# A loop moved between the two halves of the last expert group, weight splits in a written order, and residual adds spread out

## The chip, the cores and the metric

The kernel runs on one core of a Trainium2 chip. The metric is device microseconds per execution. The matmul engine is called PE, the vector engine DVE, the scalar engine ACT, GpSimd POOL, and SP is the engine that issues the transfers.

## The reference

Two transformer blocks on a sequence of 256 tokens of width 1024 (16 meta tokens are put in front for the first one and dropped at its end), in float32:

```python
x = first_block(x, meta_tokens, ...)   # layer norm, mixer, layer norm, experts, layer norm
return second_block(x, positions, ...) # two layers: attention and pooling, each with an MLP
```

The first block's mixer runs a gated delta rule (4 heads, chunks) and a stick-breaking attention (8 heads) side by side, gates and merges them. Its expert layer has 4 groups of 8 experts; each token goes to 2 experts of its best group, with two up matrices (1024 x 256) and one down matrix (256 x 1024) per expert, and the weighted results are added to the residual before a layer norm. The second block's first layer is attention: RMS norm, qkv product, rotation, causal softmax, output product; an MLP with squared ReLU follows (1024 to 4096 and back), then a pooling layer and a second MLP, and a last RMS norm.

## The kernel before

**Precision.** Most weights are used as two float32r numbers, a high part (ACT casts the raw weights, line 310) and a low part (DVE subtracts the high part from the raw weights, line 312), and the activations likewise (xh, xl); a product is then three matmuls: high by high, low by high, high by low (lines 360 to 362 with weights stationary, 388 to 390 with activations stationary, 372 to 400 for the versions that take all high parts first). The helper `split_into` (line 309) makes both parts. `Stream.split` (line 327) does it for a half of a 1 MB chunk: 1024 columns. `Stream.load` keeps up to N_RING = 5 chunks in flight or in store; SP issues the transfers in the order of the program. `Stream.after` may hold an instruction that the low part is to come behind. `tc.issue_after(i)` adds an edge: what is written inside comes after i on i's engine. Beyond such edges and the data's own, the compiler sets each engine's order, by the order of the text, and lets later work go ahead where it expects an engine to be idle.

**Mixer.** `delta()` (inverses of triangular matrices by `invert`, line 608: POOL masks a copy of the matrix, PE multiplies twice, DVE updates X and XT), `fill()` (the projections, one block of weights per step) and `stick()` are generators, and a loop steps them in rounds, counted by `it` (line 1016). At round 2 it writes `router_weights()` (line 952; two products of 128x288 on POOL, four matmuls on PE at line 960, small sums on DVE), at round 12 `residual_rows()` (line 557; four adds and products of 128x1024 on DVE that scale the residual by the embedding norm's gain and bias, line 561). `mark["POOL"]` is the last first product of an inverse, `mark["DVE"]` the last update of an XT; both blocks are queued behind the mark of their engine.

**Experts.** The experts' weights come as 99 chunks of 1 MB into 22 slots; a slot's next load is issued when the chunk in it has been used. There are 8 groups of 4 experts with 32 tokens each. Per group (loop from line 1425): eight chunks give gate and up (line 1441), ACT and DVE form the hidden rows, PE transposes them (line 1470), hT is copied out, and four chunks give the down products in two halves of 512 columns (line 1417). `weighted` (line 1393) scales a half by the router's weight into a high part on ACT (line 1398) and a low part on DVE (line 1400), in one buffer each; `scatter` (line 1403) adds it to the four accumulators on PE (line 1407). Experts with more than 32 tokens have further blocks. One is done in the middle, with its own weights; the others are done in a loop of the program whose count is read on the chip (`n_ext`), line 1480. In front of the last group's down products PE does WARM2 = 18 matmuls on the identity (line 483), then comes the loop, then both halves. All engines meet at the loop, and what is written behind it starts behind it. With these inputs its count is zero.

**Changeover.** Behind the last scatter PE does WARM3 = 10 matmuls on the identity; DVE takes the statistics of the accumulators (lines 446, 447), an inverse root (lines 413 to 422), ACT and DVE normalise (lines 1527, 1528), PE transposes (line 1553), ACT writes xh (line 1557), ACT and DVE in turn x (lines 1098 and 1096), DVE xl (line 1559). The second block's weights are taken in with `wpost.ahead()` (line 1537): five chunks are loaded and two halves split, the low parts behind the last normalised row `rows2`. The first quarter of qkv takes two halves with `xs_front` (line 392: all high parts first, 16 matmuls at line 400, then 8 with the low parts) and two with `xs_half`.

## Time and profile before

| | |
|---|---|
| median of 3 runs | 1025.97 us (1024.57 to 1027.17) |
| the profiled execution | 1022.95 us, span of its instructions 1021.2 us |
| PE busy | 945.9 us, 93% of the span |
| DVE, ACT, POOL busy | 590.5, 449.5, 71.0 us |
| moved by DMA | 227.39 MB, 223 GB/s on average |

The rows below are from that profiled execution. In a chain of waits each step is followed back from the last instruction to what released it; "issue" is time in which an engine waited for nothing that the profile shows. In a timeline, the bracket is the idle time of the engine ahead of the instruction and what ended it. The granted clock is a share of full speed, 2.4 GHz.

### The profile page before, as it was taken

Reading aid. Unit: us, or ns where it says so; the run is one execution under the profiler, and the core shown is the slowest. Engines: PE = TensorE matmul, PEld = TensorE weight load, DVE = VectorE, ACT = ScalarE, POOL = GpSimd, SP = SyncE. Lnnn points to the kernel's source line nnn. Section 1 sums busy time; section 2 is a strip of 40 time slices with the busy share of each in tenths; the row PEclk is TensorE's granted clock in tenths of the full one; section 3 lists DMA queues with packets and bytes.
Section 4 is the critical chain, followed back from the end, with each engine's and each line's share of the span. In section 5 each row is a group of like instructions: output and inputs, shape, how many; then the busy total and the mean of one; then the engine's idle time right before and its main releaser. Section 6 shows DMA issues by size and latency. Waiting matters only on the chain.

```text
span 1021.2 us, 15933 instructions
## 1 busy us (share of the span) xinstructions
PE 945.9 (93%) x6447; PEld 780.5 (76%) x6447; DVE 590.5 (58%) x1141; ACT 449.5 (44%) x771; POOL 71.0 (7%) x62
## 2 busy tenths in 40 slices
PE   6987998999999888888879999999999989999996
PEld 5986987899884523334367889999999889999995
DVE  7975757684764311122276777655565686565654
ACT  4943655344432111111154665544444464445442
POOL 0014232000300000000020001000000020000002
PEclk9998999999999999999989999999999999999999
DMA  9521212749779999999865534555455525555521
GB/s 361 188 96 42 83 43 83 287 163 348 305 298 381 416 426 422 427 422 426 340 234 186 178 122 164 190 172 201 169 202 173 198 84 206 173 199 171 200 83 41
DMA packets 34236, 227.39 MB, mean 223 GB/s; under 512 B 3937, under 2 KB 4705, under 8 KB 7665
## 3 DMA queue, kind: packets, MB, share of 16 engines
q1 hardware_dynamic: 34160, 226.36, 58.1%
q8 instruction: 51, 0.84, 0.3%
q14 instruction: 25, 0.20, 0.1%
HBM read 225.29 MB, written 1.05 MB: 222 GB/s over the span
## 4 chain that ended last, share of the span: by engine, by line
PE 72%; DVE 10%; DMA 10%; ACT 4%; POOL 2%; issue 2%; SPq 0%; POOLq 0%; ACTq 0%; DVEq 0%
DMA wexp<-in_wexp_dram 10%; PE bank L362 10%; PE bank L361 9%; PE bank L360 9%; PE acc L1763 5%; PE acc L1764 5%; PE acc L1765 5%; PE bank L1441 3%; DVE wsplit L312 3%; PE bank L389 3%; PE bank L390 2%; PE bank L388 2%; PE bank L1223 2%; PE bank L1417 1%; PE bank L636 1%
## 5 line engine op out<-in xcount | busy, mean ns | idle before, releaser
L312 DVE TENSOR_TENSOR wsplit<-wraw,wsplit 128x1024 fp32r<-128x1024 f32 x222 | 277.6, 1251 | 165.3 <-ACT wsplit L310 165.2
L310 ACT CAST wsplit<-wraw 128x1024 fp32r<-128x1024 f32 x222 | 231.9, 1045 | 153.0 <-PE acc L1765 90.9
L362 PE MATMUL bank<-xl,wsplit 128*128 128x256 f32 x512 | 143.7, 281 | 3.5 <-DVE xl L1543 3.5
L361 PE MATMUL bank<-xh,wsplit 128*128 128x256 f32 x512 | 143.1, 280 | 0.0
L360 PE MATMUL bank<-xh,wsplit 128*128 128x256 f32 x512 | 143.1, 280 | 0.0
L1763 PE MATMUL acc<-wsplit,mhh 128*128 128x512 f32 x256 | 100.4, 393 | 0.0
L1764 PE MATMUL acc<-wsplit,mhh 128*128 128x512 f32 x256 | 99.8, 390 | 0.0
L1765 PE MATMUL acc<-wsplit,mhl 128*128 128x512 f32 x256 | 99.7, 390 | 0.0
L362 PEld LDWEIGHTS bank<-xl,wsplit 128*128 128x128 f32 x512 | 96.4, 188 | 4.3 <-DVE xl L1543 4.3
L361 PEld LDWEIGHTS bank<-xh,wsplit 128*128 128x128 f32 x512 | 96.3, 188 | 0.5
L360 PEld LDWEIGHTS bank<-xh,wsplit 128*128 128x128 f32 x512 | 96.3, 188 | 0.5
L360 PE MATMUL bank<-hh,wsplit 128*128 128x256 f32 (+1 forms) x304 | 88.7, 292 | 0.0
L361 PE MATMUL bank<-hh,wsplit 128*128 128x256 f32 (+1 forms) x304 | 86.9, 286 | 0.6 <-DVE wsplit L312 0.6
L362 PE MATMUL bank<-hl,wsplit 128*128 128x256 f32 (+1 forms) x304 | 86.5, 285 | 0.0
L1753 ACT ACTIVATE relu<-bank 128x256 f32<-128x256 f32 x64 | 24.5, 383 | 85.5 <-PE bank L362 85.5
L1441 PE MATMUL bank<-wexp,xt 128*32 128x512 f32 x512 | 62.2, 598 | 0.0
L361 PEld LDWEIGHTS bank<-hh,wsplit 128*128 128x128 f32 x304 | 57.4, 189 | 1.1 <-DVE wsplit L312 0.8
L360 PEld LDWEIGHTS bank<-hh,wsplit 128*128 128x128 f32 x304 | 57.5, 189 | 0.3 <-issue 0.2
L362 PEld LDWEIGHTS bank<-hl,wsplit 128*128 128x128 f32 x304 | 57.3, 189 | 0.0
L1765 PEld LDWEIGHTS acc<-wsplit,mhl 128*128 128x128 f32 x256 | 48.0, 188 | 10.1
L1764 PEld LDWEIGHTS acc<-wsplit,mhh 128*128 128x128 f32 x256 | 48.1, 188 | 9.9 <-DVE wsplit L312 0.3
L1763 PEld LDWEIGHTS acc<-wsplit,mhh 128*128 128x128 f32 x256 | 48.1, 188 | 9.6
(535 smaller groups left out, 1635.6 us busy)
## 6 DMA issues: line engine op xcount, KB each, us to landing
wexp<-in_wexp_dram SPq DMA_DIRECT2D x99, 1024.0 KB, 19.5
wraw<-in_wpost_dram SPq DMA_DIRECT2D x81, 1024.0 KB, 4.7
wraw<-in_wpre_dram SPq DMA_DIRECT2D x30, 1024.0 KB, 4.9
h<-in_x_dram SPq DMA_DIRECT2D x2, 512.0 KB, 4.2
eb<-in_rowv_dram SPq DMA_DIRECT2D x2, 512.0 KB, 11.2
out_dram<-of SPq DMA_DIRECT2D x4, 256.0 KB, 2.1
cpre<-in_cst_dram SPq DMA_DIRECT2D x1, 915.5 KB, 10.4
pmat<-in_poolm_dram SPq DMA_DIRECT2D x1, 544.0 KB, 3.6
```

What stands on the lines that cost most here:

```text
L310: S.copy(hi, src)
L312: (sub or V).tensor_tensor(lo, src, hi.bitcast(F32), op=OP.subtract)
L360: PE.matmul(p[:, :width], wh[:, o:o + 128], xh[:, k, :], start=k == 0, stop=False)
L361: PE.matmul(p[:, :width], wl[:, o:o + 128], xh[:, k, :], start=False, stop=False)
L362: PE.matmul(p[:, :width], wh[:, o:o + 128], xl[:, k, :], start=False, stop=k == nk - 1)
L388: PE.matmul(banks[c], xh[:, k, tsl], w1, start=k == 0, stop=False)
L389: PE.matmul(banks[c], xh[:, k, tsl], w2, start=False, stop=False)
L1441: PE.matmul(pg[32 * e:32 * e + 32, :], xt[:, k, 32 * e:32 * e + 32], w[:, e, :], start=k == 0, stop=k == 7)
L1753: S.activation(t, p[:, :SEQ], AF.Relu)
L1763: PE.matmul(ac[c][n], hh_, wh, start=g == 0 and k == 0, stop=False)
L1764: PE.matmul(ac[c][n], hh_, wl, start=False, stop=False)
L1765: PE.matmul(ac[c][n], hl_, wh, start=False, stop=g == 7 and k == 3)
```

## The change

Seven edits. (1) The loop for further blocks, with its warm-up, moves from in front of the last group's first down half to between the halves; inside its body one buffer gets another tag. (2) WARM2 goes from 18 to 8, WARM3 from 10 to 16. (3) `split_into` takes two marks, one for the high and one for the low part. (4) At the start of the second block five chunks are loaded but none split; four halves are split inside the loop that makes xh, x and xl: the high parts of the first two behind the last scaling of an expert result (`mark["ACT"]`), of the other two behind the fourth xh, the low parts behind the second, fourth, sixth and eighth xl. (5) The two router products go from POOL to DVE and lose their mark. (6) The residual adds become four steps, one in each round from 8 on, each behind `mark["DVE"]`. (7) `mark["POOL"]` is gone.

```diff
--- before.py
+++ after.py
@@ -35,8 +35,8 @@
 HEADS = "32 s0 36 s1 42 s2 p0 44 s3 p1 46 s4 50 s5 p2 52 v0 p3 s6 54 s7 v1 p4 56 v2 p5 60 v3 p6 p7 v4 v5 v6 v7"
 WARM0 = 10
 WARM = 14
-WARM2 = 18
-WARM3 = 10
+WARM2 = 8
+WARM3 = 16
 PAD = 32
 N_LAST1 = 2
 N_LAST2 = 4
@@ -306,9 +306,10 @@
         nc.sync.dma_start(t, dram[i])
         return t
 
-    def split_into(hi, lo, src, sub=None, after=None):
-        S.copy(hi, src)
-        with tc.issue_after(after.ins) if after else nullcontext():
+    def split_into(hi, lo, src, sub=None, after=(None, None)):
+        with tc.issue_after(after[0].ins) if after[0] else nullcontext():
+            S.copy(hi, src)
+        with tc.issue_after(after[1].ins) if after[1] else nullcontext():
             (sub or V).tensor_tensor(lo, src, hi.bitcast(F32), op=OP.subtract)
 
     class Stream:
@@ -316,7 +317,7 @@
 
         def __init__(self, dram, n_chunks, g_halves=(), extra={}, still=()):
             self.g_halves, self.extra, self.depth, self.still = g_halves, extra, 2, still
-            self.after = None
+            self.after = (None, None)
             self.dram, self.i, self.n, self.raw, self.q, self.got = dram, 0, n_chunks, [], [], 0
 
         def load(self, n):
@@ -524,9 +525,9 @@
     for i, src in enumerate(rows):
         n = src.shape[0]
         front = rescale(src, src, mv3[:n, i, 0:1], r3[:n, i:i + 1], i == 1)
-    wpre.after = front
+    wpre.after = (None, front)
     wpre.split()
-    wpre.after = None
+    wpre.after = (None, None)
     pk = [bank("pk") for _ in range(4)]
     pm = bank("pk")
     for c in range(2):
@@ -559,6 +560,9 @@
         for c in range(2):
             for q in range(2):
                 V.tensor_tensor(h0[:, c, :], h0[:, c, :], eb[:, q, :], op=OP.add if q else OP.mult)
+                yield
+
+    residual_steps = residual_rows()
 
 
     wab = mix.tile([128, 288], F32R, tag="At0", name="wab")
@@ -613,7 +617,7 @@
         w3 = lambda t: t.rearrange("p (h d) -> p h d", d=128)
         bc = lambda m: C(m)[:, None, :].to_broadcast([128, n, 128])
         t0 = mix.tile([128, W], F32, tag=f"inv_t{n}", name="inv_t", bufs=2)
-        mark["POOL"] = G.tensor_tensor(w3(t0), w3(At), bc("lev1"), op=OP.mult)
+        G.tensor_tensor(w3(t0), w3(At), bc("lev1"), op=OP.mult)
         V.tensor_tensor(w3(XT), bc("ident"), w3(t0), op=OP.subtract)
         yield
         p = bank()
@@ -955,7 +959,7 @@
         k36 = lambda a: a.rearrange("p (k n) -> p k n", n=36)
         for q, n in enumerate(("ln1g", "ln1b")):
             o = _VCOLS[n][0]
-            G.tensor_tensor(k36(t[:, q, :]), k36(wrt), colv[:, o:o + 8, None].to_broadcast([128, 8, 36]), op=OP.mult)
+            V.tensor_tensor(k36(t[:, q, :]), k36(wrt), colv[:, o:o + 8, None].to_broadcast([128, 8, 36]), op=OP.mult)
             p = bank()
             PE.matmul(p[:, :288], C("ones"), t[:, q, :], start=True, stop=True)
             V.tensor_reduce(rcb[:, q, :], p[:, :288].rearrange("p (k n) -> p n k", n=36), axis=AX.X, op=OP.add)
@@ -1015,11 +1019,10 @@
     it = 0
     while m_on or f_on or sticks:
         if it == 2:
-            with tc.issue_after(mark["POOL"].ins):
-                router_weights()
-        if it == 12:
+            router_weights()
+        if it >= 8:
             with tc.issue_after(mark["DVE"].ins):
-                residual_rows()
+                next(residual_steps, None)
         it += 1
         if m_on:
             m_on = next(M, "end") != "end"
@@ -1330,7 +1333,7 @@
         V.tensor_copy(pm, pp[:CAP, :SEQ])
         return xx, pm
 
-    def spare_block(xx, pm, weights):
+    def spare_block(xx, pm, weights, loop=False):
 
         pg = bank2()
         for k in range(8):
@@ -1346,7 +1349,7 @@
         hT = rt([2, CAP], "xhT")
         S.copy(hT.rearrange("p q s -> p (q s)"), pt[:, :2 * CAP])
         for n in range(2):
-            ys = moe.tile([128, 512], F32, tag="ys" + "hl"[n], name="xys")[:CAP]
+            ys = moe.tile([128, 512], F32, tag="xt" if loop else "ys" + "hl"[n], name="xys")[:CAP]
             w = weights(4 + n)
             py = bank2()
             for q in range(2):
@@ -1366,7 +1369,7 @@
             spare_weights(t, eg, ej, 2 * i, 2)
             return t
 
-        spare_block(xx, pm, weights)
+        spare_block(xx, pm, weights, True)
 
 
     first, place = [], []
@@ -1395,7 +1398,7 @@
         yh = moe.tile([128, 512], F32R, tag="ysh", name="ysh")
         yl = moe.tile([128, 512], F32R, tag="ysl", name="ysl")
         for sl, p in parts_:
-            S.activation(yh[:, sl], p, AF.Copy, scale=Pw)
+            mark["ACT"] = S.activation(yh[:, sl], p, AF.Copy, scale=Pw)
         for sl, p in parts_:
             V.scalar_tensor_tensor(yl[:, sl], p, Pw, yh[:, sl].bitcast(F32), op0=OP.mult, op1=OP.subtract)
         return yh, yl
@@ -1471,14 +1474,6 @@
         hT = moe.tile([128, 2, 128], F32, tag="hT", name="hT")
         evac(hT, pt[:, :256].rearrange("p (q s) -> p q s", s=128))
         full, hf = slice(0, 512), (slice(0, 256), slice(256, 512))
-        if g == NG - 1:
-
-            warm(WARM2)
-            wx = slot()
-            with tc.issue_after(last_load[0].ins):
-                n_x = nc.values_load(n_ext[0:1, 0:1], min_val=0, max_val=14)
-            with tc.For_i(0, n_x, 1):
-                overflow(wx)
         py = bank2()
         for i in range(2):
             down(py, full, hT, chunk(), i)
@@ -1492,6 +1487,13 @@
             flush()
             pend.append((g, 1, Pm, weighted([(full, py)], Pw)))
         else:
+
+            warm(WARM2)
+            wx = slot()
+            with tc.issue_after(last_load[0].ins):
+                n_x = nc.values_load(n_ext[0:1, 0:1], min_val=0, max_val=14)
+            with tc.For_i(0, n_x, 1):
+                overflow(wx)
             py = [bank2()[:, :256], bank2()[:, :256]]
             for i in range(2):
                 w = chunk()
@@ -1533,9 +1535,7 @@
     post = ctx.enter_context(tc.tile_pool(name="post", bufs=1, reuse_waits="tile"))
     cvp.append(ctx.enter_context(tc.tile_pool(name="cvt2", bufs=2, reuse_waits="tile")))
     wpost = Stream(A["wpost"], 81, still=STILL)
-    wpost.after = rows2
-    wpost.ahead()
-    wpost.after = None
+    wpost.load(N_RING)
 
     def scaled(x, k, gname, xh, xl):
 
@@ -1554,10 +1554,16 @@
                      h0[:, c, k * 128:(k + 1) * 128], ident)
     pk = [pk[k // 2][:, (k % 2) * 256:(k % 2 + 1) * 256] for k in range(8)]
     for k in range(8):
-        S.activation(xh[:, k, :], pk[k], AF.Identity, bias=gb2[:, 1, k:k + 1], scale=gb2[:, 0, k:k + 1])
+        x3 = S.activation(xh[:, k, :], pk[k], AF.Identity, bias=gb2[:, 1, k:k + 1], scale=gb2[:, 0, k:k + 1])
         affine(k + 1, x[:, k, :], pk[k], col("ln2g", k), col("ln2b", k))
-        V.scalar_tensor_tensor(xl[:, k, :], x[:, k, :], col("nmix0", k), xh[:, k, :].bitcast(F32),
-                               op0=OP.mult, op1=OP.subtract)
+        low = V.scalar_tensor_tensor(xl[:, k, :], x[:, k, :], col("nmix0", k), xh[:, k, :].bitcast(F32),
+                                     op0=OP.mult, op1=OP.subtract)
+        if k % 2:
+            wpost.after = (mark["ACT"] if k < 4 else high, low)
+            wpost.split()
+        if k == 3:
+            high = x3
+    wpost.after = (None, None)
     dump("h2", x)
     if stop <= 2:
         return
```

## Rows read from the trace of the kernel before

**Rows 1.** Windows by stage, all engines: busy us (instructions), granted clock, DMA share, GB/s.
```profile
60.00:306.00 246.00, 233.31 (x1747) 215.91 (x1751) 158.26 (x311) 116.40 (x194) 47.69 (x38) 0.97 0.46 176
306.00:503.00 197.00, 171.54 (x1204) 76.00 (x1196) 50.97 (x148) 29.20 (x63) 0.00 (x0) 1.00 0.99 411
503.00:538.00 35.00, 25.28 (x145) 18.99 (x146) 22.23 (x43) 18.72 (x29) 6.83 (x4) 0.90 0.67 255
538.00:1021.00 483.00, 468.92 (x3008) 425.00 (x3006) 307.11 (x515) 245.86 (x402) 15.53 (x12) 1.00 0.46 163
```

**Rows 2.** Waits of PE, 60 to 306 us: total, times, longest us.
```profile
PE bank L960 <- POOL wr L958: 5.6, 1, 5.6
PE bank L636 <- ACT inv_u L632: 3.7, 2, 3.3
```

**Rows 3.** Chain of waits around the router weights: start us, us, what.
```profile
86.20 2.40 PE bank L960 x4
...
90.73 1.32 PE bank L621 x9
```

**Rows 4.** Timeline of DVE, 84 to 92 us: start, us, instruction, idle before.
```profile
85.55 1.14 DVE L617 TENSOR_TENSOR XT<-cst,inv_t 128x512 f32<-128x512 f32 x1 [0.84 <-POOL inv_t L616]
...
88.38 1.21 DVE L312 TENSOR_TENSOR wsplit<-wraw,wsplit 128x1024 fp32r<-128x1024 f32 x1
...
90.87 0.46 DVE L964 TENSOR_TENSOR wrt<-wr,rcb 128x288 f32<-128x288 f32 x1
```

**Rows 5.** Line L561, the residual adds: ns min/median/max, first and last start.
```profile
L561 DVE TENSOR_TENSOR h<-h,eb x4: 1210/1640/2314, 154.8 to 161.3; 128x1024 f32<-128x1024 f32 x4
```

**Rows 6.** Chain of waits behind the residual adds.
```profile
164.21 1.01 DVE sbwork L884 x2
```

**Rows 7.** Timeline of DVE, 130 to 156 us.
```profile
146.16 1.02 DVE L889 SCALAR_TENSOR_TENSOR sbwork<-sbwork 128x832 f32<-128x832 f32 x1 [4.47 <-ACT sbwork L887]
```

**Rows 8.** Chain of waits, 290 to 540 us.
```profile
481.56 21.26 DMA wexp<-in_wexp_dram
502.82 1.39 issue
504.21 3.65 PE bank L1417 x48
...
510.34 0.75 ACT ysh L1398 x2
...
514.22 1.09 DVE wsplit L312
...
520.21 2.27 DVE wsplit L312 x2
...
523.84 5.98 PE bank L400 x18
```

**Rows 9.** Timeline, 498 to 524 us, all engines.
```profile
498.51 4.18 PE L483 MATMUL bank<-cst 128*128 128x128 f32 x36
498.72 0.42 DVE L1092 COPY hT<-bank 128x256 f32<-128x256 f32 x1 [0.53 <-PE bank L1470]
...
505.95 1.43 PEld L1417 LDWEIGHTS bank<-wexp,hT 128*32 128x32 f32 x28 [0.30 <-issue]
...
506.20 0.69 ACT L1398 ACTIVATE ysh<-bank,pwt 128x512 fp32r<-128x512 f32 x1 [8.47 <-PE bank L1417]
506.92 0.75 DVE L1400 SCALAR_TENSOR_TENSOR ysl<-bank,pwt,ysh 128x512 fp32r<-128x512 f32 x1 [7.78 <-ACT ysh L1398]
...
508.35 1.99 ACT L310 CAST wsplit<-wraw 128x1024 fp32r<-128x1024 f32 x2 [1.46 <-DMA wraw<-in_wpost_dram]
```

**Rows 10.** Windows of PE in the changeover: busy us (instructions), granted clock, DMA share.
```profile
512.00:514.00 2.00, 2.00 (x8) 0.50 1.04 438
...
524.00:528.60 4.60, 4.60 (x14) 0.63 0.80 328
528.60:536.00 7.40, 7.40 (x34) 1.00 0.14 24
```

## What the change is predicted to do

> **What bounds the kernel now.** I read the stretches by stage first, to see which engine or queue each stage has to wait for [rows 1]. In the first block's mixer (60 to 306 us) PE is busy 233 of 246 us, the DMA less than half. In the expert stage (306 to 503) the DMA share is 0.99 and PE has 25 us to spare. In the changeover to the second block (503 to 538) PE is busy 25.3 of 35 us and the DMA share is 0.67, so neither fills it. From 538 on PE is busy 469 of 483. So time won before 306 is kept: the 22 slots for expert weights are full by then, and the next loads start when the first expert matmul frees one; the weights' stream, which fills the next 197 us, moves with that matmul. Inside the expert stage nothing can be won on an engine. In the changeover everything won is kept, as PE has hardly a gap behind it.
>
> Then the waits of PE in the mixer: two hold 8.9 us, the four products of the router weights (L960) that wait 5.6 us for POOL's L958, and L636 that waits 3.3 us for ACT [rows 2]. Last the chain of waits of the changeover [rows 8]: the last expert weights land at 481.56 + 21.26 = 502.82; 1.39 us "issue" is the loop for further blocks, which runs no time here; PE does all down products behind it; and then the chain runs over casts and subtractions of second-block weights (L310, L312) that nothing needs yet.
>
> **The change, part by part.**
>
> *Router weights (mixer).* The two products go from POOL, behind the inverses' first products, to DVE, free in order. PE did L960 at 86.20 and reached the next block of matmuls at 90.73 + 1.32 = 92.05 [rows 3]. What is late next: the transposes of XT (L621) need L617, done at 86.7, and the block's low weights need L312, done at 89.6 [rows 4]. L617 took 1.14 us next to POOL and its wait for POOL ended at 85.55, so with POOL free the transposes can end about 88.2, and L312 is done between 88.4 and 89.6. Two products on DVE cost about 2 x 0.46 us (estimate by the 128x288 product L964 [rows 4]). Bounds: 0 (the products stall PE as long elsewhere) to 5.6 us; I take 2.3, since L312 is the nearest thing that holds.
>
> *Residual rows (mixer).* The same four adds of 128x1024, 1.21 to 2.31 us each, 6.8 us in all (1.21 + 2 x 1.64 + 2.31), stood together from 154.8 to 162.5 [rows 5], and the chain passes through them to L884 at 164.21 [rows 6], then over the stick's ACT and POOL steps to PE's 3.3 us wait. Now one stands behind each of four earlier rounds, where DVE has holes such as the 4.47 us before 146.16 [rows 7]: costed at nothing by that cover, up to 4 x 1.1 us if they meet POOL's products instead. L884 can come up to 3 us sooner. Bounds 0 to 3.3; I take 2.3. Mixer: 4.6 us.
>
> *Loop between the halves.* hT is there at 498.72 + 0.42 = 499.14, but PE does the warm-up (36 instructions in 4.18 us) and waits for the loop [rows 9]. The first half's products take 505.95 - 504.21 = 1.74 us; now they run before the loop, while the last chunk is still landing. That chunk, 502.82, and the loop's 1.39 us remain [rows 8]. The loop is a wait for all engines, so behind it in each queue stand SP's five weight loads (as before), and now in front of it stand the scaling and the subtraction of the first half, 0.69 + 0.75 us [rows 9]. With the half's products first on PE they end at 499.14 + 1.74 + 0.25 (from the products to ACT, 505.95 to 506.20) + 1.44 = 502.6, before the landing: free. With the eight warm-up matmuls (16 x 0.116 us) first, at about 504: the loop passes 1.1 us later. I take 0 and keep -1.1. Gain 1.7.
>
> *Casts in a written order.* After the loop, ACT's two casts (L310) waited for the first second-block weights and ran 508.35 to 510.34; the second half's scaling followed them at once [rows 8, 9], though its buffer was free by about 508.8 (estimate: the first half's subtraction ends at 507.67 [rows 9], and four matmuls of some 0.25 us read its result). Now the casts stand behind that scaling: 1.5 us (bounds 0 to 2.0). They still wait for the same landing, and behind them on ACT stands the normalisation, needed at about 513; the casts end at 510.4, and cover it with 2 us to spare. The scatter of the second half then follows without PE's pause; it ran at a granted clock of 0.50 [rows 10]: 0.4 us (0 to 0.8).
>
> *Low parts.* Two subtractions (1.09 us each, the first at 514.22) stood between the statistics and the reciprocal root: 2.2 us. Two more, 2.27 us from 520.21, stood ahead of the first x rows: 2.0 us [rows 8]. All four are now written behind the second, fourth, sixth and eighth xl. There they lengthen DVE's work for x and xl by 4.5 us. PE's first quarter of qkv is 48 matmuls at 7.40/34 = 0.218 us [rows 10], 10.5 us; it could go on only at 523.84, with the first xl [rows 8], and ended at 536, 13.5 us after the first x row could start (520.21 + 2.27 = 522.5). Now it takes at least 12.5 (10.5, and some 2 until the first two rows are made) and at most 18 (13.5 and all four low parts). The low clock of 524 to 528.6 cost 4.6 x 0.37 = 1.7 us of the old 13.5 [rows 10] and should go, so I take 14.3: -0.8 (bounds +1 to -4.5). WARM3 at 16 ends some 3.7 us behind the scatter, just as the first transposes are ready: 0 (-1.6 if the clock is low).
>
> The tuple argument, the buffer name in the loop's body and the load of five chunks without splits change nothing that runs here: the first split keeps its edge, the body is not entered, and the same five loads leave behind the same loop.
>
> Sum of the changeover: 1.7 + 1.5 + 0.4 + 2.2 + 2.0 - 0.8 = 7.0 us. With the mixer 11.6 us: 1022.95 - 11.6 = 1011.35 us for the profiled execution, whose span is 1021.2 us. That execution is 3.0 us below the median of the runs, 1025.97; from the median the forecast is **1014.4 us**.
>
> **A rule against the row.** One and the same add takes 1.21 to 2.31 us [rows 5]. The Trainium skill, SBUF — State Buffer, section "SBUF: two separate sides", says that a DVE operation with two SBUF inputs and a POOL operation hold the shared ports in turn, each blocking the other for a whole instruction; that spread fits it. What it would make of the change is rival B.
>
> **The rivals.**
>
> B. *The mixer gives little.* Products and adds on DVE meet POOL's L616 and L626; each meeting costs 0.9 to 1.1 us in the inverse's chain, and PE's two waits only move. Four or five of them leave about 1 us of the 4.6: 1025.97 - 7.0 - 1.0 = 1018.0. For it: the add's two lengths. Against: DVE's holes.
>
> C. *The changeover gives little.* The loop passes 1.1 us late, behind the first half's scaling, and the four low parts between the xl hold PE for their whole 4.5 us: 7.0 - 5.6 = 1.4 us are left: 1025.97 - 4.6 - 1.4 = 1020.0. For it: PE already waited for xl at 523.84. Against: the first 16 matmuls need only high parts.
>
> D. *Slower: the clock.* The granted clock, 1.00 in 528.6 to 536, was 0.63 in the stretch before [rows 10], after PE had waited for the normalisation. With 8 in place of 18 warm-up matmuls PE can come out of the loop at 0.5. The Trainium skill, TensorE: Matmul & The Clock Gate, section "What's actually happening", says that low is the resting state and only activity lifts it; the row agrees. At half rate the first half (1.7), the second (1.9), eight scatter matmuls (2.0), the transposes (2.0) and the first quarter (10.5) cost another 18.1 us, less the 2.7 that low clock cost before (2.0 x 0.5 + 4.6 x 0.37): 15.4 - 11.6 = 3.8 us slower, 1029.8. It decides only if the clock stays at 0.5 through 536; a short spell costs 1 or 2 us.
>
> E. *The order isn't what the text says.* An edge only says what an instruction comes after; the compiler may put other casts or the products where they hold as before. Then only the moved half's 1.7 us are left: 1024.3.
>
> **How the numbers follow.** Forecast 0.55, B 0.18, C 0.12, D 0.06, E 0.09. What a measurement can tell from no change is 0.3%, 3.1 us: under 1022.9 is faster, over 1029.0 slower. Faster 0.55 + 0.18 + 0.12 = 0.85, same 0.09, slower 0.06. The forecast's own range is 1009 to 1018 (mixer up to 8.9 us, changeover up to 10, not both at their ends); with B and C inside it is 1009 to 1021.5.
>
> **What would show it.** Right: PE's waits for L958 and before L636 each under 1 us and the first expert matmul 4 to 5 us earlier; the first half's products before the loop; the second half's scaling with no L310 ahead; no L312 between statistics and root; first x row some 7 us sooner after the last landing; PE at full clock from the first quarter on. Wrong: a wait of PE for DVE in 80 to 150 us in place of POOL's; the last landing no earlier; DVE's last xl later than 13 us after the first x row; a clock of 0.5 in the first quarter.

## The result: 1014.33 us, a ratio of 0.990

The changed kernel took 1014.33 us (median of 4 runs, 1013.32 to 1017.42) beside 1025.27 us for the kernel before (4 runs). The ratio is 0.9896, with an interval of 0.9868 to 0.9923: 10.7 us less, beyond the 0.3% that a measurement can tell. Six more runs of the same kernel, on the chip of the last experiments, gave 1017.44 us and 0.9926 (0.9908 to 0.9944), 7.6 us less. All ten have a median of 1017.1 us. The range (1009 to 1021.5) holds for both groups. That the first median lies 0.1 us from the forecast of 1014.4 is luck: the median of all ten lies 2.7 us above it, and two terms were off in opposite directions.

**The profile after.** The profiled execution took 1015.25 us, its span 1013.5. First the windows by stage, all engines, as in [rows 1]:

```profile
60.00:301.00 241.00, 230.09 (x1751) 213.04 (x1755) 159.82 (x314) 116.64 (x195) 46.33 (x36) 0.99 0.48 180
301.00:498.00 197.00, 171.34 (x1200) 74.10 (x1192) 50.98 (x148) 29.32 (x63) 0.00 (x0) 1.00 0.99 411
498.00:526.00 28.00, 19.90 (x130) 14.46 (x126) 21.40 (x41) 17.33 (x28) 5.39 (x4) 1.00 0.65 252
```

The mixer is 5 us shorter, the expert stage as long as before, and the changeover up to the products of the root ends 28 us behind the expert stage, not 35 (these products also stand ten matmuls earlier on PE than before, as told below). The mixer's waits of PE, 60 to 306 us (total, times, longest us), against [rows 2]:

```profile
PE bank L625 <- DVE XT L621: 3.8, 2, 3.1
PE bank L640 <- ACT inv_u L636: 2.1, 2, 1.5
```

PE no longer waits for POOL's router products; 3.8 us came back as two waits for XT, the thing named as late next. (The same list also has 3.9 us for `krow`. That is no loss of the change: the longest of these waits, 2.6 us, is as long in the kernel before and ends there at 59.0 us, just outside the window.) Of the 3.3 us ahead of L636 (now L640) 0.61 us are left at that place; the rest of the 2.1 is an earlier wait that grew from 0.4 to 1.5 us; the account of the residual rows comes back to it.

The timeline of the changeover (start, us, instruction, idle before), against [rows 8, 9]:

```profile
494.31 1.07 PE L1420 MATMUL bank<-wexp,hT 128*32 128x512 f32 x8 [0.52 <-DVE hT L1095]
495.31 2.05 PE L484 MATMUL bank<-cst 128*128 128x128 f32 x16
497.29 1.07 PE L1420 MATMUL bank<-wexp,hT 128*32 128x512 f32 x8
498.47 0.69 ACT L1401 ACTIVATE ysh<-bank,pwt 128x512 fp32r<-128x512 f32 x1 [5.62 <-PEq L1495]
499.19 0.75 DVE L1403 SCALAR_TENSOR_TENSOR ysl<-bank,pwt,ysh 128x512 fp32r<-128x512 f32 x1 [4.93 <-ACTq L1495]
500.70 0.49 PE L1410 MATMUL acc<-ysh,Pm 128*128 128x512 f32 x1 [2.35 <-DVEq L1495]
...
503.76 0.84 ACT L1401 ACTIVATE ysh<-bank,pwt 128x256 fp32r<-128x256 f32 x2 [4.60 <-PE acc L1410]
...
506.10 1.99 ACT L311 CAST wsplit<-wraw 128x1024 fp32r<-128x1024 f32 x2 [1.50 <-DMA wraw<-in_wpost_dram]
...
510.04 1.52 DVE L1530 TENSOR_SCALAR h<-acc,mv,rs_y 128x512 f32<-128x512 f32 x2
```

The last expert weights land at 498.03. The first half's products run before the loop, as written, but the 16 warm-up instructions stand between their two steps: the half ends 2 us later than need be, DVE's subtraction ends at 499.94, and PE leaves the loop 2.68 us behind the landing; before, it was 1.39 [rows 8]. The second half's scaling then runs with no cast ahead, and no low part stands between statistics and normalisation.

What comes next, on DVE (timeline) and on POOL (timeline):

```profile
512.34 1.00 DVE L1099 TENSOR_SCALAR x<-bank,colv 128x256 f32<-128x256 f32 x2 [0.78 <-ACT xh L1557]
...
514.88 1.23 DVE L313 TENSOR_TENSOR wsplit<-wraw,wsplit 128x1024 fp32r<-128x1024 f32 x1
...
520.94 1.21 DVE L313 TENSOR_TENSOR wsplit<-wraw,wsplit 128x1024 fp32r<-128x1024 f32 x1
522.08 1.50 DVE L1559 SCALAR_TENSOR_TENSOR xl<-x,colv,xh 128x256 fp32r<-128x256 f32 x1
523.50 3.94 DVE L313 TENSOR_TENSOR wsplit<-wraw,wsplit 128x1024 fp32r<-128x1024 f32 x2
```
```profile
519.41 1.33 POOL L1579 TENSOR_TENSOR acc<-sq 128x512 f32<-128x512 f32 x1 [250.74 <-ACT sq L1574]
521.79 1.51 POOL L1579 TENSOR_TENSOR acc<-acc,sq 128x512 f32<-128x512 f32 x1 [1.05 <-ACT sq L1574]
523.38 1.33 POOL L1587 TENSOR_TENSOR acc<-acc,sq 128x512 f32<-128x512 f32 x1
524.78 1.58 POOL L1589 TENSOR_TENSOR acc<-acc 128x256 f32<-128x256 f32 x1
```

DVE has no hole from the first x row on. In the compiled order its fourth low part, at 520.94, is that of the fifth half of weights; the fourth half's, which the first quarter needs, is the one at 523.50. Beside POOL's sums a low part takes up to 2.28 us (the first of the two at 523.50) in place of 1.23, and an xl 1.50 in place of 0.48. PE's wait for POOL's sums (497 to 545 us; first the kernel before, then the changed one) and its windows in the changed kernel (busy, granted clock, DMA share, GB/s):

```profile
PE bank L1596 <- POOL acc L1583: 1.1, 1, 1.1
```
```profile
PE bank L1602 <- POOL acc L1589: 3.8, 1, 3.8
```
```profile
513.00:522.70 9.70, 9.25 (x38) 1.00 0.72 258
526.50:530.60 4.10, 4.10 (x13) 0.58 0.88 302
530.60:536.00 5.40, 5.40 (x25) 1.00 0.64 220
```

The compiler put the root's four products ten matmuls earlier than before (behind 38 of the quarter's 48), PE waits 3.75 us there for POOL's sums, and behind the wait it runs at a granted clock of 0.58: another 4.1 x 0.42 = 1.7 us. In the kernel before, the last of POOL's sums stands in the chain of waits as

```profile
535.61 1.60 POOL acc L1583
```

It ends at 537.21, 14.8 us behind the first x row (522.40); in the changed kernel the sums end at 526.36, 14.0 us behind it. So the sums came no later behind that row. PE came sooner: its 38th matmul is done 10.3 us behind the row, and there it has to wait.

### The profile page after: what moved, and what is told of

Its sections match the earlier page's. It is cut to its first block, busy times and chain, and to the rows that moved or that the text cites. A ratio compares the mean times of both kernels' runs of the same rounds, so it can differ in the third digit from the quotient of the medians.

```text
span 1013.5 us, 15919 instructions
## 1 busy us (share of the span) xinstructions
PE 941.8 (93%) x6439; PEld 775.4 (77%) x6439; DVE 593.1 (59%) x1143; ACT 449.1 (44%) x771; POOL 68.3 (7%) x60
## 4 chain that ended last, share of the span: by engine, by line
PE 45%; DVE 3%; ACT 2%; POOL 0%; issue 0%; ACTq 0%; DVEq 0%
PE bank L363 7%; PE bank L362 6%; PE bank L361 6%; PE acc L1769 6%; PE acc L1770 6%; PE acc L1771 6%; PE bank L391 2%; PE bank L390 2%; PE bank L389 2%; DVE wsplit L313 1%; ACT wsplit L311 1%; DVE xl L1543 0%; PE bank L1648 0%; PE bank L1612 0%; PE bank L1659 0%
## 6 DMA issues: line engine op xcount, KB each, us to landing
cpre<-in_cst_dram SPq DMA_DIRECT2D x1, 915.5 KB, 10.3
```

## The experiments

All medians, in the order run (10 runs where no number is given); "before" was 1025.25, 1024.5 and 1025.44 us beside the three groups of four.

| run | median us (runs) | ratio to before | interval |
|---|---|---|---|
| mix_only | 1018.89 (10) | 0.9939 | 0.9920 to 0.9959 |
| chg_only | 1022.35 | 0.9970 | 0.9952 to 0.9988 |
| loop_only | 1022.56 | 0.9976 | 0.9957 to 0.9995 |
| order_only | 1022.88 | 0.9978 | 0.9964 to 0.9992 |
| root_later | 1017.49 (6) | 0.9923 | 0.9907 to 0.9939 |
| warm_last | 1016.12 (6) | 0.9929 | 0.9905 to 0.9953 |
| both | 1015.35 (5) | 0.9908 | 0.9894 to 0.9923 |
| no_warm | 1015.69 (4) | 0.9906 | 0.9887 to 0.9925 |
| all_three | 1014.82 (6) | 0.9897 | 0.9879 to 0.9915 |
| after_again | 1017.44 (6) | 0.9926 | 0.9908 to 0.9944 |
| router_only | 1022.95 (10) | 0.9968 | 0.9948 to 0.9989 |
| resid_only | 1020.47 (5) | 0.9956 | 0.9932 to 0.9981 |

One kernel's runs lie 2.6 to 8.2 us apart, so the traces have to tell single terms. This table is read from one trace each: the first expert matmul and the last expert weights' landing (us from the start), and, in us behind that landing, where PE leaves the loop, the first x row (DVE), the first product with pT in the second block's attention (PE), and the end.

| trace | first expert matmul | landing | loop left | first x row | pT | end |
|---|---|---|---|---|---|---|
| before | 305.61 | 502.82 | 1.39 | 19.58 | 93.04 | 518.37 |
| after | 300.73 | 498.03 | 2.68 | 14.31 | 90.52 | 515.42 |
| after_again | 300.58 | 497.88 | 2.69 | 14.31 | 90.45 | 515.59 |
| mix_only | 302.88 | 499.98 | 1.53 | 19.25 | 91.86 | 516.97 |
| chg_only | 307.58 | 505.90 | 1.63 | 13.26 | 89.41 | 514.53 |
| loop_only | 305.51 | 502.18 | 3.34 | 19.71 | 90.90 | 515.99 |
| order_only | 308.38 | 506.24 | 0.74 | 13.90 | 90.09 | 514.98 |
| root_later | 304.56 | 502.43 | 2.04 | 13.69 | 89.69 | 514.78 |
| both | 302.47 | 500.15 | 1.47 | 12.65 | 89.76 | 515.38 |
| all_three | 300.22 | 497.55 | 1.68 | 12.87 | 88.62 | 513.75 |
| warm_last | 297.31 | 494.41 | 6.93 | 18.12 | 94.33 | 519.94 |
| no_warm | 300.69 | 498.32 | 4.00 | 17.55 | 92.33 | 517.47 |
| router_only | 306.36 | 504.25 | 0.74 | 20.31 | 92.41 | 517.58 |
| resid_only | 301.87 | 499.15 | 3.55 | 21.29 | 93.88 | 519.55 |

**The mixer's edits alone.**

```diff
-            G.tensor_tensor(k36(t[:, q, :]), ...)
+            V.tensor_tensor(k36(t[:, q, :]), ...)
...
-        if it == 12:
+        if it >= 8:
             with tc.issue_after(mark["DVE"].ins):
-                residual_rows()
+                next(residual_steps, None)
```

> Only the mixer's edits (router products on DVE, residual adds one per round); the changeover stays as before. Theory: they give about 4.6 us, kept through the expert stage: 1025.3 - 4.6 = 1020.7 us, the first expert matmul 4 to 5 us earlier than in the trace before, and the changeover from the last landing on as long as before. Rival: most of the 4.9 us between the two traces is chance of the granted clock in the first 25 us and in the router stage: then 1.5 to 2.5 us, 1023 to 1024, with PE's 5.6 us wait replaced by waits for XT.

6.2 us by the ratio (0.0061 x 1025.25), 4.2 to 8.2 by its interval: the theory's mechanism, and by the median more than its 4.6, which the interval still holds.

**The changeover's edits alone** (loop between the halves, warm-ups, written order of the splits; the two runs below divide it).

```diff
-    wpost.after = rows2
-    wpost.ahead()
+    wpost.load(N_RING)
...
+        if k % 2:
+            wpost.after = (mark["ACT"] if k < 4 else high, low)
+            wpost.split()
```

> Only the changeover's edits (loop between the halves, new warm-up counts, written order of the splits); the mixer as before. Theory: 7.0 us less what the changed trace shows to be given back, 2.7 us more of PE's wait for the second block's root sums: about 5 us, 1020.5, the span from the last landing to the end of the first quarter some 6 us shorter. With the mixer's part it adds up to the whole change (10.9 us). Rival: the two parts don't add, as the mixer's gain is chance: then this one alone gives 9 or more, 1016.

3.1 us (1.2 to 4.9): under the 5 expected here, under the prediction's 7.0, and well under the rival's 9. The first x row comes 6 us sooner behind the landing than before, but at pT 3.6 us are left of it.

**The loop's move and the warm-ups alone.**

```diff
-WARM2 = 18
-WARM3 = 10
+WARM2 = 8
+WARM3 = 16
...
-        if g == NG - 1:
-            warm(WARM2)
...
         else:
+            warm(WARM2)
```

> Only the loop between the halves with the new warm-up counts; the first splits as before (in the compiler's order). Theory: the first half's 1.74 us leaves the path, but the loop waits for its scaling and passes 1.2 us later, and the casts still hold ACT in front of the second half's scaling: 0 to 1 us, 1024.3 to 1025.3. Rival: the moved half is worth its full 1.7 us or more: 1023 or less.

2.5 us. The median is the rival's, but not by a sooner second half: PE leaves the loop 1.95 us later behind the landing than before, and the first x row is not earlier (19.71 against 19.58). The gain stands behind that row, where the profile shows no wait of PE for xl and none for the root. Matmul by matmul against the trace of before, 0.9 us come at the first weights of the quarter, but the three traces with the old changeover (mix_only, router_only, resid_only) have those too; another 1.4 us come at the root's products, where POOL's sums end 11.9 us behind the first x row, not 14.8. Why they end sooner there stays open.

**The order of the splits alone.**

```diff
+        with tc.issue_after(after[0].ins) if after[0] else nullcontext():
+            S.copy(hi, src)
+        with tc.issue_after(after[1].ins) if after[1] else nullcontext():
```

> Only the written order of the first four splits; the loop in front of both halves and the old warm-up counts. Theory: casts and low parts leave the chain: 1.5 + 2.2 + 2.0 us, of which the wait for the root sums takes back about 2.5: 3 to 4 us, 1021.5 to 1022.3. Rival: without the moved loop the order gives nothing, since ACT then waits for the first landing in any case: 1024.5 or more.

2.3 us (0.8 to 3.7), a little under the theory's smallest gain. The first x row comes 5.7 us sooner; then PE waits 3.79 us at the root's products, as in the changed kernel. So this wait belongs to the written order, not to the loop's move.

**The root's products ten matmuls later.**

```diff
-                xs_half(wpost, k0, 8, xh, xl, pb)
+                done = xs_half(wpost, k0, 8, xh, xl, pb)
...
-                rs[:] = rstd_columns(acc)
+                with tc.issue_after(done.ins): rs[:] = rstd_columns(acc)
```

> The changed kernel, with one edge more: the four products that sum the squares for the second block's root come behind the last matmul of the quarter's step before, ten matmuls later on PE, at the place that they have in the kernel before. In the trace of the changed kernel PE waits 3.75 us for POOL's sums at these products and its matmuls behind them run 0.43 us apart for some 4 us. Theory (this wait is where the changeover's gain is given back): the ten matmuls of 0.22 us fill 2.2 us of the wait, about 1.5 us of it stay, and the spell at the low clock (1.7 us) goes with it or shrinks: 1010.4 to 1012.1 us against 1014.3 for the changed kernel. Rival (the wait is only in front of the next limit, the evictions that need the root): PE waits behind the products instead, 1014 to 1016 us.

The median says no gain and lies above both ranges expected. PE's waits, 497 to 545 us, and a window of PE in that run:

```profile
PE bank L390 <- DVE wsplit L313: 3.2, 1, 3.2
```
```profile
529.60:534.50 4.90, 4.90 (x16) 0.65 0.80 264
```

The wait at the root is gone, and PE stands nearly as long at its 39th matmul, for the fourth half's low part on DVE; the low clock follows again. The root was not the bound: DVE's work stands right beside POOL's (the low part ends 13.4 us behind the first x row, the sums 14.0), and the theory's 2.2 to 3.9 us fall.

**The warm-up behind the half's last product; and both edges.**

```diff
-            warm(WARM2)
+            with tc.issue_after(mark["PE"].ins): warm(WARM2)
```

> The changed kernel with the warm-up behind the first half's last product, where the text has it; in the trace of the changed kernel it stands between the two steps of that half (2.05 us), the half ends at 498.36, its subtraction on DVE at 499.94, and PE leaves the loop 2.67 us behind the last landing, 1.28 us later than before the change. Theory: the half ends about 2 us sooner, the loop waits for the landing alone and is left some 1.4 us behind it: 1.2 to 1.3 us gained, 1013.0 us. Rival (the loop's passing is hidden anyway, or PE loses the same in clock because the warm-up now ends while PE waits): 1014.3 us, no change; in that case PE's work behind the loop starts sooner and the first x row does not.

> The changed kernel with both edges, the later root products and the warm-up behind the first half's last product. Theory: the two gains stand in different stretches and add: 2.2 to 3.9 and 1.2 us, so 1009.2 to 1010.9 us, the fastest of all these kernels. Rival: the sooner loop only lengthens the wait for POOL's sums or the other way round, and one of the two gains is lost: 1012 to 1013 us.

Both lie above what was expected, and neither median separates from the changed kernel's. (The trace of the first has a spell of half clock in the expert stage, told of in the last section, so its loop is left late.) In the trace with both, the loop is left 1.47 us behind the landing and the first x row comes 1.66 us sooner than in the changed kernel (12.65 against 14.31). Not all of this is the edge: without it the loop is left 7.3 us behind the last hidden rows' transposes, with it 6.4 to 6.5, whenever the weights land, so the edge is worth 0.8 to 0.9 us and not 1.2. The warm-up itself now stands last ahead of the loop: PE's first matmul behind the loop comes 1.5 to 1.6 us after its end. More than half of the 1.66 us is lost again at once: PE waits 3.2 us for the low part as above, and the clock stays low for longer, in the window of PE

```profile
526.30:532.00 5.70, 5.70 (x16) 0.50 0.79 276
```

**No warm-up in the changeover.** Both counts 0; matmuls on the identity are left out that nothing reads.

> The changed kernel without the two warm-ups of the changeover (8 at the loop, 16 behind the scatter; their matmuls write nothing that is read). Theory (the price of rival D is a short spell): PE comes out of the loop at the low clock and the second half (1.9 us), the scatter (2.0 us) and the transposes (2.0 us) run at half rate until the clock rises; less the 2.05 us of warm-up that stood ahead of the loop: 2 to 5 us slower than the changed kernel, 1016 to 1019 us. Rival (as D was priced, low clock through the first quarter): 1026 us or more. A third outcome, 1014 us or less, would say that the warm-ups buy nothing here.

1015.69 us: in none of the three ranges, 0.3 us under the theory's and 1.7 over the third outcome. Beside the changed kernel's 1014.33 and 1017.44 no price shows. The windows of PE show the low clock and how short it is:

```profile
503.00:508.00 5.00, 4.34 (x36) 0.66 0.92 341
508.00:514.00 6.00, 1.30 (x4) 0.69 1.01 426
514.00:518.00 4.00, 3.94 (x19) 0.61 0.73 303
518.00:526.00 8.00, 7.00 (x31) 1.00 0.56 197
```

From 518 on, with the first quarter hardly begun, the clock is full. Behind the landing the trace is 1.8 us later at pT than the changed kernel; against the spread of runs that is nothing measurable. The run doesn't price the warm-ups alone. Its last hidden rows' transposes come 196.4 us behind the first expert matmul, not 192.6, after a spell of half clock in the expert stage, and its loop is left only 5.2 us behind them, not 7.3. Its compiled order differs too: the root's products stand behind all 48 matmuls, PE waits 2.24 us there, and behind that wait the clock stays full. So from the first x row to pT it takes 74.8 us, 1.4 less than in the changed kernel.

**All three edges.** Beside both edges above, the fifth half's cast and low part come last; `LOW[1]` is the last square and `LOW[0]` the low part of the fourth half:

```diff
-        mean_square(x, k, acc)
+        with tc.issue_after(x3.ins) if k == 5 else nullcontext():
+            mean_square(x, k, acc)
+    wpost.after = (LOW[1], LOW[0])
```

> The changed kernel with the later root products and the late warm-up (as in the run with both), and one order more: the cast and the low part of the fifth half of second-block weights, which the compiler put between the seventh and the eighth xl, ahead of the low part of the fourth half, come behind the last square and behind that low part; the third square comes behind the eighth xh, where it stood. In the run with both PE waits 3.2 us for the fourth half's low part, and half the clock is granted for some 6 us behind the wait. Theory (what gives the changeover's gain back is DVE's work behind the first x row, and the order in it): the fourth low part starts 1.2 us sooner and runs clear of some of POOL's sums (2.28 us beside them, 1.2 alone), so the wait shrinks by 1.2 to 2.2 us and the low clock by up to 2 us: 1011.2 to 1014.1 us against 1015.35. Rival (PE waits for the next low part or for POOL's sums by as much, or the clock falls as before): 1014.5 to 1016 us, no difference.

DVE's timeline, and PE's waits, 497 to 545 us:

```profile
518.14 1.54 DVE L1561 SCALAR_TENSOR_TENSOR xl<-x,colv,xh 128x256 fp32r<-128x256 f32 x2
519.60 1.22 DVE L315 TENSOR_TENSOR wsplit<-wraw,wsplit 128x1024 fp32r<-128x1024 f32 x1
521.17 4.10 DVE L315 TENSOR_TENSOR wsplit<-wraw,wsplit 128x1024 fp32r<-128x1024 f32 x2 [0.35 <-ACT wsplit L313]
```
```profile
PE bank L1604 <- POOL acc L1591: 2.5, 1, 2.5
```

The fourth half's low part now runs 9.2 us behind the first x row, not 11.2, and takes 1.22 us. PE no longer waits for it; it has done all 48 matmuls where it waits for POOL's sums, 2.5 us. pT comes 1.1 us sooner behind the landing than with both, 1.9 sooner than in the changed kernel. So the theory holds for the wait that it named, and the rival for what came next: most of it is now the wait for the sums, and the low clock behind it is as in the changed kernel (0.58 for 4.1 us). The median, 1014.82 us, is in the rival's range; it is 2.6 us below the changed kernel's in the same group, but the intervals of the two ratios overlap, so it is the fastest of that group and not shown to be faster.

**The changed kernel once more.** No edit.

> The changed kernel once more, unaltered, for more runs of it beside the others. If its gain of 10.7 us (four runs, interval 7.9 to 13.5) is what the traces add up to, 1014 to 1016 us; if the runs with one edge more (1015.35 to 1017.5) truly lost time, it stays at 1014.3 or under and below them; if they only drew from the same spread, it comes out between 1015 and 1016.5 us. First expert matmul by the traces of six kernels with the mixer's change: 297.3 to 304.6 us.

1017.44 us: above all three expectations. The trace is the same as the first (300.58 and 14.31 against 300.73 and 14.31), so the first four runs drew from the lower part of the spread, and the runs with one edge more lost nothing.

**Each of the mixer's edits alone** (the two hunks above).

> The kernel before with the two router products on DVE, free in order, and nothing else. Theory: PE's wait of 5.6 us for POOL's L958 goes, and about 3.5 us of it come back as a wait for DVE's L617 and the transposes behind it: 2.1 to 2.3 us, 1023.0 us; PE's wait ahead of L636 (3.3 us) stays. Rival B: PE waits as long at 80 to 150 us, 1024.5 to 1026 us.

> The kernel before with the four residual adds one to a round and nothing else. Theory: PE's wait ahead of L636 falls from 3.3 to under 1 us, 2.3 to 2.7 us, and some of the spell of low clock behind it (0.88 granted over 176 to 190 us) goes too: 1021.0 to 1023.0 us. Rival B: the adds meet POOL's products and lengthen the inverses' chain by 1 us each: 1024.5 to 1026 us.

3.3 us (0.0032 x 1025.44) and 4.5 us, each with an interval of 2 us or more either way; their sum, 7.8, is above the 6.2 of both together, within these intervals. PE's waits of 60 to 306 us, first with the router products alone, then with the residual rows alone:

```profile
PE bank L621 <- DVE XT L617: 3.8, 2, 3.1
PE bank L636 <- ACT inv_u L632: 3.7, 2, 3.3
```
```profile
PE bank L963 <- POOL wr L961: 5.6, 1, 5.6
...
PE bank L639 <- ACT inv_u L635: 0.6, 1, 0.6
```

Each edit takes away its own wait and leaves the other. The clock tells why the second is worth more than its wait. PE's window from 174 to 190 us in the kernel before, with the router products alone, and with the residual rows alone:

```profile
174.00:190.00 16.00, 13.16 (x70) 0.89 0.38 135
```
```profile
174.00:190.00 16.00, 12.73 (x62) 0.79 0.35 122
```
```profile
174.00:190.00 16.00, 15.39 (x97) 1.00 0.53 186
```

With PE's wait of 3.3 us goes the low clock behind it: 16 x 0.11 = 1.8 us at 0.89, 16 x 0.21 = 3.4 at 0.79.

## Why the prediction was right, and where it was not

**The total** was right, and by terms that erred both ways: the mixer gave more than its 4.6 us, the changeover 2.5 to 3.1 (the two traces, and the ratio of its edits alone) and not 7.0.

**Router products, 2.3 us.** Right in mechanism and size. L617 was named as late next, and the wait for XT is there. Laid matmul by matmul against the trace of before, the offset just ahead of the products taken off, PE is 2.4 to 2.5 us sooner behind them in eight of the nine traces with this edit (1.8 in both); by the ratio it is 3.3 with a wide interval.

**Residual rows, 2.3 us.** Right in mechanism, undersized. The wait shrank by 3.28 - 0.61 = 2.7 us, and the term counted the wait alone; the 1.8 us of low clock behind it had no place in the sum: the wait is in [rows 2], and the window behind it is in no row. Matmul by matmul PE is 4.2 us sooner behind this wait in all nine traces with this edit, so the low clock is worth 1.5 to 1.8 of it. So the mixer came to 5.6 us by the first expert matmul (mean of the four traces without both edits 306.8, of the eight with them 301.2); counted from the waits for `krow` near 60 us, since the traces lie up to 3 us apart ahead of them, it is 247.1 against 240.9, 6.2 us, as the ratio says.

The cover held in part. The four adds took 1.20, 1.22, 1.22 and 2.06 us, but the first meets POOL's product L898, and a low part of weights stands right behind it on DVE. POOL and DVE there, first in the changed kernel, then in its second trace, which has the same code:

```profile
125.89 3.92 POOL L898 TENSOR_TENSOR sbwork<-sbwork 128x832 f32<-128x832 f32 x1 [12.69 <-DVE sbwork L897]
```
```profile
126.75 1.22 DVE L313 TENSOR_TENSOR wsplit<-wraw,wsplit 128x1024 fp32r<-128x1024 f32 x1
```
```profile
125.65 2.78 POOL L898 TENSOR_TENSOR sbwork<-sbwork 128x832 f32<-128x832 f32 x1 [12.69 <-DVE sbwork L897]
```
```profile
126.51 3.00 DVE L313 TENSOR_TENSOR wsplit<-wraw,wsplit 128x1024 fp32r<-128x1024 f32 x1
```

In the first, POOL ends 1.84 us behind the low part, having waited for the add and for it, and PE's wait ahead of L640 grows by 1.1 us (0.39 to 1.52). In the second, POOL ends 1.83 us behind the add, the low part takes 3.00 us, and PE's wait stays at 0.4. Four of the nine traces with this edit go the first way, five the second. So the one meeting that cost PE anything is the kind that rival B had priced (0.9 to 1.1 us); its four or five, 3.6 us in all, did not come, and as a forecast B fell.

**Kept behind the mixer.** Right: from the first expert matmul to the last landing it is 196.7 to 198.3 us in all fourteen traces. But the reason given, that PE has 25 us to spare in the expert stage, was too generous: in most traces the last hidden rows' transposes come 192.6 us behind the first expert matmul, some 5 us before the landing. Where the profile shows PE at half clock for a while (below), that margin is gone.

**Loop between the halves, 1.7 us, and its passing at 0.** With the half's 1.7 us and the casts' 1.5 the second scaling should have started 7.43 - 3.2 = 4.2 us behind the landing; it started at 5.73. The failed step is the choice of 0 between 0 and -1.1: the compiler put the warm-up inside the half, where the forecast had the products first, and PE left the loop 1.29 us later, most of the missing 1.5. Some 0.8 to 0.9 us of it are the warm-up's place, by the runs with the late warm-up; the rest is the warm-up itself, which even there ends only 1.5 to 1.6 us before PE leaves the loop. (The lower bound was also too small by its own terms: 502.6 + 16 x 0.116 is 504.4, 1.6 us behind the landing and not 1.1.)

**Low parts, 2.2 + 2.0, and scatter 0.4.** From the second scaling to the root's first step 6.18 us became 4.01, so 2.2 of 2.6; from there to the first x row 5.97 became 4.57, 1.4 of 2.0. With the above the first x row comes 5.3 us sooner behind the landing, not 7.8.

**First quarter, -0.8 us.** This is the step that failed most. From the first x row to pT, 73.46 us before became 76.21, and 72.7 is the mean of before, mix_only, router_only and resid_only: 2.8 to 3.5 us lost, not 0.8. The term counted PE's 48 matmuls, the xl and the low parts; POOL's sums of the squares, which PE needs for the root, had no place in it. The low clock at the quarter's start did go, and PE was through 38 matmuls 10.3 us behind the first x row; but the sums end 14.0 us behind that row (before 14.8, in the three others with the old changeover 13.4 to 13.9), and the fourth low part ends at 13.4 on a DVE without a hole. So PE waited 3.75 us, the low clock came back behind that wait, 1.7 us, and the 48 matmuls ended 18.7 us behind the row in place of 14.3. The bound of -4.5 held the loss; the value taken did not. Rival C had named the loop 1.1 us late and the low parts holding PE; it priced the changeover at 1.4 us left, and 2.5 to 3.1 is nearer to C than to the forecast. It missed the order in which the low parts came, and the sums on POOL.

**Rival D** fell: without any warm-up the clock is full from 518 us on, at the start of the first quarter, and the median doesn't move. **Rival E** was right in two places (the warm-up inside the half; the fifth half's low part ahead of the fourth's), but the casts and the low parts went where the text says.

**A rule and the rows.** DVE's subtraction of 128x1024 took 1.23 us and 2.28 beside POOL's sums; the second of POOL's adds took 1.51 us, and 2.21 in the run with all three edges. The Trainium skill, SBUF — State Buffer, section "SBUF: two separate sides", has a two-input DVE operation and a POOL operation lock the shared ports in turn for whole instructions; the rows agree. So do the two traces of one code above: POOL's product and DVE's subtraction take 3.92 and 1.22 us in one, 2.78 and 3.00 in the other. The prediction weighed this for the mixer in rival B and left it out of the changeover.

## What to carry to other kernels

A wait of PE can cost more than itself: here a low clock stood behind the waits of 3.3, 3.75 and 5.6 us, and none behind one of 2.24. Price both from the windows behind the waits, when one is removed and when one may come. When work that stood ahead of a stage is moved into it, look for every engine that may then end last (here POOL's sums and DVE's fourth low part, within 1 us of each other), and ask in which order the compiler will place the moved pieces: an edge says what they come after, not what may pass them. And read single terms from traces against a common mark such as the last landing, when runs of one kernel lie as far apart as the terms.

## What the runs showed of the hardware

The granted clock differs between executions where the code and its order are the same. In PE's window of 320 to 350 us, in the expert stage, it was 1.00 in the changed kernel (first fence) and 0.78 in the run with the late warm-up (second fence), whose edit stands far behind:

```profile
320.00:350.00 30.00, 27.09 (x212) 1.00 1.02 415
```
```profile
320.00:350.00 30.00, 27.16 (x172) 0.78 1.02 416
```

There PE reached the last hidden rows 197.6 us behind the first expert matmul, not 192.6, and that the first expert matmul came 3.4 us sooner than in the changed kernel was of no use. Two more traces have it (0.83 without warm-ups, 0.89 with the residual rows alone), and before 22 us some traces have a spell at half clock and others none. The clock fell behind a stretch in which PE had hardly a hole, as PE's windows of the run with the late warm-up show (first fence). At the same matmuls, 3.4 us later in the changed kernel, PE was as busy and the clock stayed full (second fence):

```profile
330.00:335.00 5.00, 4.95 (x40) 1.00 1.02 416
335.00:340.00 5.00, 5.00 (x32) 0.65 1.01 388
```
```profile
333.40:338.40 5.00, 4.95 (x40) 1.00 1.02 416
338.40:343.40 5.00, 4.19 (x34) 1.00 1.01 392
```

Why one execution falls there and another doesn't stays open. The Trainium skill, TensorE: Matmul & The Clock Gate, section "What's actually happening", says that the number of slow matmuls at a kernel's start differs from run to run of the same kernel. The spells before 22 us agree with it; the spell in the middle of the expert stage is shown by the traces alone.
